# Attention over more than 1024 keys: the second map's first half takes its exponential by its own maximum

## The chip, the cores and the metric

The kernel runs on one core of one Trainium2 chip. The metric is the device time of one execution in microseconds; the kernel before is given by the median of three runs. One further execution was taken by the hardware profiler, and every duration below comes from that one.

## The reference

One inference step of a small decoder, for a prompt of 2048 tokens and 8 samples of 8 tokens with cached keys and values. Layer 0 is a pooling mixer beside differential attention, layer 1 is gated linear attention. The change is in the prompt's differential attention. Per head (4 of them) and block of 128 queries, with two query/key maps of 64 dimensions and values of 128:

```python
sc = jnp.einsum('bqhcd,bkhcd->bhcqk', qi, k)              # c: the two maps
sc = jnp.where((qpos[:, None] >= kpos[None, :])[None, None, None], sc, -jnp.inf)
p = jax.nn.softmax(sc, axis=-1)
a = p[:, :, 0] - lam_full * p[:, :, 1]
return jnp.einsum('bhqk,bkhe->bqhe', a, v)
```

The result is normalised per head, multiplied by a gate and projected. A softmax row is the same whatever number is taken from the scores before the exponential, so long as sum and exponentials use the same one. All of it is fp32; products are split in parts for accuracy.

## The kernel before

The attention works in units: one query tile t of 128 queries (0 to 15) and one head h. A unit's keys are nk = 128 (t + 1). `scores` makes the two maps c = 0 and 1 of a unit, `pv` transposes the combined map and multiplies it by the values, two units later. `units` runs over t and, within it, over the heads of a stage. There are three stages: head 0 while the pool branch's output projection fills in (names zp), head 1 while the samples' attention fills in (ssc, stp, spo), heads 2 and 3 together while the attention's output projection and layer norm fill in (otp, op, oyp). `weave` hands out a stage's main work and its fill in a fixed proportion. The order of the instructions on each engine is then set at build time, by a scheduler that replays the program with its own costs and takes what is ready by priority. The score products, the maxima and the exponentials are written at a raised priority. On the chip each engine runs its list strictly in that order.

A unit is short up to t = 7 (nk at most 1024): each map has at most one PSUM tile. From t = 8 on it is long: each map comes in two halves i = 0 and 1, each a tile `sc` of two PSUM banks. There are two such tiles in all (pool `psc`), used in turn, so a half's products (L561, L562) can begin only when the exponential of the half two places earlier has read its tile. Before the change a long unit does for each map: products of half 0, its negated maximum (L566, VectorE), products of half 1, its maximum, the smaller of the two negated maxima (L579), then the exponential of both halves with that one number (L581, ScalarE), each with its row sum, and the sum of the two row sums (L584). After the second map, the factor c2 = -lambda s1 / s2 is made (L588, L589) and the maps are combined by one instruction over all nk columns, e0 + c2 e1 (L590). `pv` then transposes 128 columns at a time (L613, tile tp), copies four of them to SBUF (L618, ScalarE, tile aT) and multiplies by the values (L606, tile po).

Other lines that are spoken of: L635 squares a unit's result for its norm (VectorE), L40 and L45 split an operand in two parts (L40 is ScalarE's copy, also of the queries qr that `load_q` fetches), L751 transposes the fill's input (loaded from `mixa` to om), L756 is VectorE's part of that operand's split, L816 and L817 are the layer norm's passes on GpSimd, L1520 is a small exponential in the samples' attention.

Of the kernel before, what the change touches and what calls it, by code (L numbers as in the profile page):

```python
# [11 lines left out]
F32 = mybir.dt.float32  # L12
# [4 lines left out]
AF = mybir.ActivationFunctionType  # L17
ALU = mybir.AluOpType
# [412 lines left out]
class Attention:  # L431
# [105 lines left out]
    def scores(self, t, h):  # L537

        nc, sm = self.nc, self.sm
        qh, ql = self.qs[h, t // 2]  # L540
        qs = slice(128 * (t % 2), 128 * (t % 2) + 128)
        nk = 128 * (t + 1)

        npc = 1 if nk <= 512 else 2 if nk <= 1024 else 4
        w = nk // npc
        nt = max(npc // 2, 1)
        nm = sm.tile([128, 2, 2], F32, tag="nm", name=f"nm{t}_{h}", bufs=4)
        s = sm.tile([128, 2, 2], F32, tag="s", name=f"s{t}_{h}", bufs=6)
        places = [self.e.pop(0) for _ in range(2)]
        es = [p.tile([128, NP], F32, tag="e", name=f"e{t}_{h}_{c}") for c, p in enumerate(places)]  # L550
        for c in range(2):
            kst, pieces = self.kst[h][c], []
            for i in range(nt):
                if npc > 1 or c == 0:
                    p = self.sc_tile(f"sc{t}_{h}_{c}_{i}")
                with self.tc.high_priority(300):
                    for j in range(min(npc, 2)):
                        k = 2 * i + j
                        o = p[:, j if npc > 1 else c, :w]
                        ks = slice(k * w, (k + 1) * w)  # L560
                        nc.tensor.matmul(o, qh[:, c, qs], kst[:, ks], start=True, stop=False)  # L561
                        nc.tensor.matmul(o, ql[:, c, qs], kst[:, ks], start=False, stop=k < npc - 1)  # L562
                        if k == npc - 1:
                            nc.tensor.matmul(o[:, w - 128:w], self.ident_b, self.mask, start=False, stop=True)
                    if npc > 1:
                        nc.vector.tensor_reduce(out=nm[:, c, i:i + 1], in_=p[:, :, :w], op=ALU.max, axis=AX.XY,  # L566
                                                negate=True)
                    elif c:
                        nc.vector.tensor_reduce(out=nm[:, :, 0], in_=p[:, :, :w], op=ALU.max, axis=AX.X, negate=True)
                if npc > 1:  # L570
                    pieces.append((c, p[:, :, :w],
                                   es[c][:, 2 * i * w:(2 * i + 2) * w].rearrange("p (g w) -> p g w", g=2)))
                if i < nt - 1:
                    yield 4 * max(w, 256) / 2.4
            if npc == 1 and c:
                pieces = [(c, p[:, c, :w], es[c][:, :w]) for c in range(2)]
            with self.tc.high_priority(300):
                if nt == 2:
                    nc.vector.tensor_tensor(out=nm[:, c, 0:1], in0=nm[:, c, 0:1], in1=nm[:, c, 1:2], op=ALU.min)  # L579
                for i, (m, p, o) in enumerate(pieces):  # L580
                    nc.scalar.activation(o, p, AF.Exp, bias=nm[:, m, 0:1],  # L581
                                         accum_out=s[:, m, i if npc > 1 else 0:][:, :1])
                if nt == 2:
                    nc.vector.tensor_tensor(out=s[:, c, 0:1], in0=s[:, c, 0:1], in1=s[:, c, 1:2], op=ALU.add)  # L584
            if c == 1:
                s1, s2 = s[:, 0, 0:1], s[:, 1, 0:1]
                c2 = sm.tile([128, 1], F32, tag="c2", name=f"c2{t}_{h}", bufs=6)
                nc.vector.reciprocal(out=c2, in_=s2)  # L588
                nc.vector.scalar_tensor_tensor(out=c2, in0=s1, scalar=self.nlam, in1=c2, op0=ALU.mult, op1=ALU.mult)  # L589
                nc.vector.scalar_tensor_tensor(out=es[0][:, :nk], in0=es[1][:, :nk], scalar=c2, in1=es[0][:, :nk],  # L590
                                               op0=ALU.mult, op1=ALU.add)
                self.e.append(places[1])
                self.cur = (es[0], s1, places[0])
            yield 2 * min(npc, 2) * max(w, 256) / 2.4
# [1195 lines left out]
```

## Time and profile before

| | us |
|---|---|
| median of 3 runs | 2233.23 (2230.89 to 2234.32) |
| profiled execution, its time | 2228.95 |
| profiled execution, its span | 2227.0 |
| long units of head 0 | 617 to 750 of the span |
| head 1 | 750 to 910 |
| short units of heads 2 and 3 | 910 to 997 |
| long units of heads 2 and 3 | 997 to 1231 |
| granted TensorE clock, mean | 0.983 |

In the profile PE is TensorE's matmul, PEld its weight load, DVE VectorE, ACT ScalarE, POOL GpSimd, SP SyncE, which issues loads. A row of the timeline gives start, duration, engine, line, operation and tiles, and in brackets how long the engine was idle before it and what released it. A row of waits gives total us, times and the longest. A row of groups gives busy us and mean ns, then idle us ahead of it. A line's row gives least, median and largest ns.

### The profile page before, as it was taken

To read this page: it belongs to the slowest core of one execution; us is meant where nothing else is said; L and a number is where in the kernel's file an instruction comes from. 1 tells how busy PE (TensorE), PEld (TensorE's weight loads), DVE (VectorE), ACT (ScalarE), POOL (GpSimd) and SP (SyncE) were. 2 spreads that over 40 slices of the span, in tenths; PEclk is the share of its full clock that TensorE was granted. 3 is DMA by queue.
4 is the path that set the end of the run, shared out by engine and by line. 5 is a ranking of instruction groups with operands and counts; after the bars stand their busy time and mean duration, and the time that the engine had idled before them with its cause. 6 is when DMAs were issued, how large, how long until landed. Compare 5 with 4: busy or idle time off the path is not lost. (4 is left out here: it accounts for less than half of the span.)

```text
span 2227.0 us, 31576 instructions
## 1 busy us (share of the span) xinstructions
PE 2116.1 (95%) x11777; PEld 1750.0 (79%) x11777; DVE 1131.5 (51%) x2326; ACT 676.3 (30%) x1398; POOL 657.7 (30%) x702
## 2 busy tenths in 40 slices
PE   8999999999999999798889899999999997999997
PEld 7888888878788777677777688888888885877776
DVE  7444511012566676896677654810100127789984
ACT  2111100111433555655565311401111124333441
POOL 0000000231454432665533400000003343555654
PEclk9999999999999999899999999999999998999999
DMA  7311133225855498653322444311211246455522
GB/s 265 123 50 41 44 92 108 71 80 165 247 166 157 143 302 275 181 148 110 102 93 76 147 149 129 129 66 52 83 69 66 81 142 208 149 168 175 168 88 73
DMA packets 202597, 288.51 MB, mean 130 GB/s; under 512 B 30818, under 2 KB 121314, under 8 KB 202434
## 3 DMA queue, kind: packets, MB, share of 16 engines
q1 hardware_dynamic: 166594, 225.30, 33.4%
q0 software_dynamic: 12688, 43.00, 5.1%
q10 hardware_dynamic: 23152, 18.09, 2.5%
q8 instruction: 95, 1.56, 0.3%
q14 instruction: 68, 0.56, 0.1%
HBM read 183.95 MB, written 102.38 MB: 129 GB/s over the span
## 5 line engine op out<-in xcount | busy, mean ns | idle before, releaser
L51 PE MATMUL pm<-xh,wh 128*128 128x512 f32 (+2 forms) x640 | 227.1, 358 | 7.1 <-ACT xh L40 6.7
L53 PE MATMUL pm<-xh,wl 128*128 128x512 f32 (+2 forms) x640 | 228.5, 357 | 0.5 <-DVE wl L45 0.5
L52 PE MATMUL pm<-xl,wh 128*128 128x512 f32 (+2 forms) x640 | 228.0, 356 | 0.6 <-DVE xl L45 0.6
L53 PE MATMUL vt<-wk,yl 128*128 128x512 f32 (+1 forms) x544 | 211.4, 389 | 0.0
L52 PE MATMUL vt<-wk,yh 128*128 128x512 f32 (+1 forms) x544 | 211.3, 390 | 0.0
L51 PE MATMUL vt<-wk,yh 128*128 128x512 f32 (+1 forms) x544 | 208.8, 390 | 0.0
L581 ACT ACTIVATE e<-sc,nm 128x896 f32<-128x896 f32 (+11 forms) x192 | 164.8, 864 | 97.9 <-DVE nm L579 65.9
L1031 POOL TENSOR_TENSOR ve<-ve,nw 128x512 f32<-128x512 f32 (+1 forms) x34 | 45.2, 1330 | 467.9 <-ACT ve L1030 467.9
L45 DVE TENSOR_TENSOR wk<-wr,wk 128x1024 fp32r<-128x1024 f32 x28 | 35.5, 1267 | 273.2 <-ACT wk L40 272.8
L566 DVE TENSOR_REDUCE nm<-sc 128x1 f32<-128x768 f32 (+7 forms) x160 | 156.5, 991 | 29.2 <-PE sc L562 20.0
L606 PE MATMUL po<-vt,aT 128*128 128x128 f32 x1088 | 156.4, 283 | 3.7 <-ACT aT L618 3.0
L397 POOL TENSOR_TENSOR et<-et,gw 128x512 f32<-128x512 f32 (+1 forms) x17 | 22.2, 1304 | 455.3 <-ACT et L396 455.3
L561 PE MATMUL sc<-kst,qh 128*128 128x512 f32 (+9 forms) x352 | 134.1, 384 | 20.7 <-ACT e L581 20.1
L606 PEld LDWEIGHTS po<-vt,aT 128*128 128x128 f32 x1088 | 140.5, 197 | 10.6 <-ACT aT L618 4.0
L51 PEld LDWEIGHTS pm<-xh,wh 128*128 128x128 f32 x640 | 120.9, 189 | 24.8 <-ACT xh L40 6.7
L52 PEld LDWEIGHTS pm<-xl,wh 128*128 128x128 f32 x640 | 120.9, 189 | 19.4 <-DVE xl L45 1.6
L53 PEld LDWEIGHTS pm<-xh,wl 128*128 128x128 f32 x640 | 120.9, 189 | 18.8 <-DVE wl L45 1.0
L562 PE MATMUL sc<-kst,ql 128*128 128x512 f32 (+9 forms) x352 | 122.4, 351 | 0.0
L52 PEld LDWEIGHTS vt<-wk,yh 128*128 128x128 f32 (+1 forms) x544 | 100.4, 185 | 23.0
L53 PEld LDWEIGHTS vt<-wk,yl 128*128 128x128 f32 (+1 forms) x544 | 100.4, 185 | 23.0
L51 PEld LDWEIGHTS vt<-wk,yh 128*128 128x128 f32 (+1 forms) x544 | 100.4, 185 | 22.9
L52 PE MATMUL qm<-yl,wk 128*128 128x512 f32 (+2 forms) x320 | 114.0, 357 | 3.3 <-DVE yl L45 3.3
(354 smaller groups left out, 5074.1 us busy)
## 6 DMA issues: line engine op xcount, KB each, us to landing
sk<-in_cachek SPq DMA_DIRECT2D x64, 256.0 KB
sv<-in_cachev SPq DMA_DIRECT2D x64, 256.0 KB
wr<-in_w_tm SPq DMA_DIRECT2D x24, 512.0 KB
wr<-in_w_fm SPq DMA_DIRECT2D x22, 512.0 KB
wr<-in_w_out SPq DMA_DIRECT2D x16, 512.0 KB
kr<-k SPq DMA_DIRECT2D x32, 256.0 KB
qr<-q SPq DMA_DIRECT2D x64, 128.0 KB
zx<-in_x SPq DMA_DIRECT2D x32, 256.0 KB
```

The lines of the kernel that those rows point to most:

```text
L45: return h, (lo_eng or nc.vector).tensor_tensor(out=lo, in0=raw, in1=hi, op=ALU.subtract)
L51: nc.tensor.matmul(ps, lh(k), rh(k), start=(first and k == 0), stop=False)
L52: nc.tensor.matmul(ps, lh(k), rl(k), start=False, stop=False)
L53: nc.tensor.matmul(ps, ll(k), rh(k), start=False, stop=(last and k == n - 1))
L397: nc.gpsimd.tensor_tensor(out=e, in0=e, in1=gw[:n], op=ALU.mult)
L561: nc.tensor.matmul(o, qh[:, c, qs], kst[:, ks], start=True, stop=False)
L562: nc.tensor.matmul(o, ql[:, c, qs], kst[:, ks], start=False, stop=k < npc - 1)
L566: nc.vector.tensor_reduce(out=nm[:, c, i:i + 1], in_=p[:, :, :w], op=ALU.max, axis=AX.XY, negate=True)
L581: nc.scalar.activation(o, p, AF.Exp, bias=nm[:, m, 0:1], accum_out=s[:, m, i if npc > 1 else 0:][:, :1])
L606: nc.tensor.matmul(po, s[:, 128 * j:128 * j + 128], vt[:, k0 + j, :], start=(k0 + j == 0), stop=(k0 + j == n - 1))
L1031: nc.gpsimd.tensor_tensor(out=e[:n], in0=e[:n], in1=nw[:n], op=ALU.mult)
```

## The change

In a long unit, the first half of the second map no longer waits for the second half's maximum. Its exponential is taken by its own maximum as soon as that is there, at the raised priority (L575 of the changed kernel). The minimum of both negated maxima goes to a third column (L584), which the other exponentials use (L586). A new exponential of one column (L591, ScalarE) makes the factor exp(m0 - m) between the two maxima; VectorE forms the second map's sum as s0 times the factor plus s1 in one instruction in place of the plain sum (L592). The factor c2 is made as before, a new product (L601) gives the first half's own c2, and the combination is done by two instructions of nk / 2 columns, each with its own factor (L604). Short units do what they did. Lines behind line 590 are 14 higher in the changed kernel.

```diff
-        nm = sm.tile([128, 2, 2], F32, tag="nm", name=f"nm{t}_{h}", bufs=4)
-        s = sm.tile([128, 2, 2], F32, tag="s", name=f"s{t}_{h}", bufs=6)
+        nm = sm.tile([128, 2, 3], F32, tag="nm", name=f"nm{t}_{h}", bufs=4)
+        s = sm.tile([128, 2, 3], F32, tag="s", name=f"s{t}_{h}", bufs=6)
...
-                    pieces.append((c, p[:, :, :w],
-                                   es[c][:, 2 * i * w:(2 * i + 2) * w].rearrange("p (g w) -> p g w", g=2)))
+                    o = es[c][:, 2 * i * w:(2 * i + 2) * w].rearrange("p (g w) -> p g w", g=2)
+                    if nt == 2 and c == 1 and i == 0:
+
+                        with self.tc.high_priority(300):
+                            nc.scalar.activation(o, p[:, :, :w], AF.Exp, bias=nm[:, c, 0:1], accum_out=s[:, c, 0:1])
+                    else:
+                        pieces.append((c, i, p[:, :, :w], o))
...
                 if nt == 2:
-                    nc.vector.tensor_tensor(out=nm[:, c, 0:1], in0=nm[:, c, 0:1], in1=nm[:, c, 1:2], op=ALU.min)
-                for i, (m, p, o) in enumerate(pieces):
-                    nc.scalar.activation(o, p, AF.Exp, bias=nm[:, m, 0:1],
-                                         accum_out=s[:, m, i if npc > 1 else 0:][:, :1])
-                if nt == 2:
-                    nc.vector.tensor_tensor(out=s[:, c, 0:1], in0=s[:, c, 0:1], in1=s[:, c, 1:2], op=ALU.add)
+                    nc.vector.tensor_tensor(out=nm[:, c, 2:3], in0=nm[:, c, 0:1], in1=nm[:, c, 1:2], op=ALU.min)
+                for m, i, p, o in pieces:
+                    nc.scalar.activation(o, p, AF.Exp, bias=nm[:, m, 2:3] if nt == 2 else nm[:, m, 0:1],
+                                         accum_out=s[:, m, i:i + 1])
+                if nt == 2 and c == 0:
+                    nc.vector.tensor_tensor(out=s[:, 0, 0:1], in0=s[:, 0, 0:1], in1=s[:, 0, 1:2], op=ALU.add)
+                elif nt == 2:
+                    nc.scalar.activation(s[:, 1, 2:3], nm[:, 1, 0:1], AF.Exp, bias=nm[:, 1, 2:3], scale=-1.0)
+                    nc.vector.scalar_tensor_tensor(out=s[:, 1, 0:1], in0=s[:, 1, 0:1], scalar=s[:, 1, 2:3],
+                                                   in1=s[:, 1, 1:2], op0=ALU.mult, op1=ALU.add)
...
-                c2 = sm.tile([128, 1], F32, tag="c2", name=f"c2{t}_{h}", bufs=6)
-                nc.vector.reciprocal(out=c2, in_=s2)
-                nc.vector.scalar_tensor_tensor(out=c2, in0=s1, scalar=self.nlam, in1=c2, op0=ALU.mult, op1=ALU.mult)
-                nc.vector.scalar_tensor_tensor(out=es[0][:, :nk], in0=es[1][:, :nk], scalar=c2, in1=es[0][:, :nk],
-                                               op0=ALU.mult, op1=ALU.add)
+                c2 = sm.tile([128, 2], F32, tag="c2", name=f"c2{t}_{h}", bufs=6)
+                last = c2[:, nt - 1:nt]
+                nc.vector.reciprocal(out=last, in_=s2)
+                nc.vector.scalar_tensor_tensor(out=last, in0=s1, scalar=self.nlam, in1=last, op0=ALU.mult, op1=ALU.mult)
+                if nt == 2:
+                    nc.vector.tensor_tensor(out=c2[:, 0:1], in0=last, in1=s[:, 1, 2:3], op=ALU.mult)
+                for i in range(nt):
+                    ks = slice(i * nk // nt, (i + 1) * nk // nt)
+                    nc.vector.scalar_tensor_tensor(out=es[0][:, ks], in0=es[1][:, ks], scalar=c2[:, i:i + 1],
+                                                   in1=es[0][:, ks], op0=ALU.mult, op1=ALU.add)
```

The scheduler answers with another order on every engine from the first long unit of head 0 to the end of the attention; ahead of that and behind it nothing moves. Three places, all where query tile 8 of head 3 ends and tile 9 of head 2 begins. In a name such as sc_3_1_0 stand head, map and half, then a running number. TensorE, first as it was and then as it is now, from the unit's last score product to the next unit's first:

```order
L564 MATMUL sc_3_1_1_10232<-mask,identb 128x128
L613 MATMUL tp_2_4_10072<-ident,e_2_0_9836 128x128 x4
L606 MATMUL po_2_10046<-vt_8234,aT_2_0_10052 128x128 x4
L751 MATMUL otp_9951<-oident,om_9947 128x128 x2
L751 MATMUL otp_9951<-oident,oq_2_9489 128x128
L751 MATMUL otp_9951<-oident,oq_3_9546 128x128
L606 MATMUL po_2_10046<-vt_8234,aT_2_4_10077 128x128 x4
L613 MATMUL tp_3_0_10150<-ident,e_3_0_9897 128x128 x4
L561 MATMUL sc_2_0_0_10260<-kst_0_8225,qh_4_9828 128x320
```

```order
L564 MATMUL sc_3_1_1_10284<-mask,identb 128x128
L627 MATMUL tp_2_4_10120<-ident,e_2_0_9884 128x128 x4
L620 MATMUL po_2_10094<-vt_8276,aT_2_0_10100 128x128 x4
L51 MATMUL op_0_9683<-wh_8824,oh_9678 128x512
L52 MATMUL op_0_9683<-wl_8825,oh_9678 128x512
L561 MATMUL sc_2_0_0_10314<-kst_0_8267,qh_4_9876 128x320
```

Less work stands between the two units than before; wide products of the fill now follow the next unit's first half. ScalarE at the same place:

```order
L618 ACTIVATE aT_2_0_10052<-tp_2_0_10047 128x512
L773 DMA y0T<-oyt_1_9774 128x4x128
L618 ACTIVATE aT_2_4_10077<-tp_2_4_10072 128x512
L581 ACTIVATE e_3_1_10138,s_3_10136<-sc_3_1_0_10205,nm_3_10135 128x576
L581 ACTIVATE e_3_1_10138,s_3_10136<-sc_3_1_1_10232,nm_3_10135 128x576
L755 ACTIVATE oh_9956<-otp_9951 128x512
```

```order
L632 ACTIVATE aT_2_0_10100<-tp_2_0_10095 128x512
L769 ACTIVATE oh_9678<-otp_9673 128x512
L575 ACTIVATE e_3_1_10189,s_3_10187<-sc_3_1_0_10256,nm_3_10186 128x576
L632 ACTIVATE aT_2_4_10125<-tp_2_4_10120 128x512
L586 ACTIVATE e_3_1_10189,s_3_10187<-sc_3_1_1_10284,nm_3_10186 128x576
L591 ACTIVATE s_3_10187<-nm_3_10186 128x1
```

The second map's first exponential now stands ahead of a copy of transposed columns that it stood behind, and the factor follows the second. VectorE, from tile 8's last maximum on:

```order
L566 TENSOR_REDUCE nm_3_10135<-sc_3_1_1_10232 128x1
L579 TENSOR_TENSOR nm_3_10135<-nm_3_10135 128x1
L584 TENSOR_TENSOR s_3_10136<-s_3_10136 128x1
L588 RECIPROCAL c_3_10243<-s_3_10136 128x1
L589 SCALAR_TENSOR_TENSOR c_3_10243<-s_3_10136,nlam,c_3_10243 128x1
L756 TENSOR_TENSOR ol_9957<-otp_9951,oh_9956 128x512
L635 SCALAR_TENSOR_TENSOR sqq_2_10101,ssq_2_9880<-oq_2_9879 128x128
L590 SCALAR_TENSOR_TENSOR e_3_0_10137<-e_3_1_10138,c_3_10243,e_3_0_10137 128x1152
L566 TENSOR_REDUCE nm_2_10256<-sc_2_0_0_10260 128x1
```

```order
L566 TENSOR_REDUCE nm_3_10186<-sc_3_1_1_10284 128x1
L770 TENSOR_TENSOR ol_9679<-otp_9673,oh_9678 128x512
L584 TENSOR_TENSOR nm_3_10186<-nm_3_10186 128x1
L566 TENSOR_REDUCE nm_2_10310<-sc_2_0_0_10314 128x1
L592 SCALAR_TENSOR_TENSOR s_3_10187<-s_3_10187 128x1
L598 RECIPROCAL c_3_10295<-s_3_10187 128x1
L599 SCALAR_TENSOR_TENSOR c_3_10295<-s_3_10187,nlam,c_3_10295 128x1
L601 TENSOR_TENSOR c_3_10295<-c_3_10295,s_3_10187 128x1
L604 SCALAR_TENSOR_TENSOR e_3_0_10188<-e_3_1_10189,c_3_10295,e_3_0_10188 128x576 x2
```

The next unit's first maximum now stands ahead of the sum, the factors and the combination, behind which it stood before.

More of the change, by code (lines that the diff above doesn't have):

```diff
@@ L575, in scores @@
             if npc == 1 and c:
-                pieces = [(c, p[:, c, :w], es[c][:, :w]) for c in range(2)]
+                pieces = [(c, 0, p[:, c, :w], es[c][:, :w]) for c in range(2)]
             with self.tc.high_priority(300):
                 if nt == 2:
-                    nc.vector.tensor_tensor(out=nm[:, c, 0:1], in0=nm[:, c, 0:1], in1=nm[:, c, 1:2], op=ALU.min)
-                for i, (m, p, o) in enumerate(pieces):
-                    nc.scalar.activation(o, p, AF.Exp, bias=nm[:, m, 0:1],
-                                         accum_out=s[:, m, i if npc > 1 else 0:][:, :1])
```

## The prediction

> **What bounds the kernel now.** I read the page first, then the busy time by stage, then the waits of TensorE in the stage that the change reaches, then single waits in the timeline.
>
> ```profile
> span 2227.0 us, 31576 instructions
> PE 2116.1 (95%) x11777; PEld 1750.0 (79%) x11777; DVE 1131.5 (51%) x2326; ACT 676.3 (30%) x1398; POOL 657.7 (30%) x702
> ```
>
> TensorE is busy for 95% of the span. The change adds and removes no matmul, so it can only give back idle TensorE time, 111 us in all, and only in the stretch in which the long score units run. Times below are us from the span's start; the columns are busy time per engine, granted clock, DMA share and GB/s.
>
> ```profile
> 617.00:750.00 133.00, 133.00 (x745) 112.55 (x744) 86.59 (x166) 50.80 (x109) 65.83 (x95) 1.00 0.50 152
> 750.00:910.00 160.00, 148.52 (x1563) 115.73 (x1562) 108.33 (x301) 93.61 (x232) 60.61 (x106) 0.99 0.82 254
> 910.00:997.00 87.00, 71.41 (x423) 57.62 (x422) 78.17 (x173) 51.89 (x129) 62.74 (x72) 0.90 0.56 162
> 997.00:1231.00 234.00, 208.09 (x1295) 177.42 (x1295) 165.69 (x364) 128.05 (x268) 116.56 (x117) 0.98 0.30 95
> ```
>
> In the first row (long units of head 0) TensorE never rests, since the pool branch's output products fill every gap: no gain there. In the second (head 1) it rests 11.5 us, in the third (short units of heads 2 and 3, whose code path the change leaves alone) 15.6 us, in the fourth (long units of heads 2 and 3) 25.9 us. So the fourth row matters, and some of the second. Who makes TensorE wait, first over the span and then in 997 to 1231:
>
> ```profile
> PE sc L561 <- ACT e L581: 20.1, 20, 3.3
> PE otp L751 <- DMA om<-mixa: 10.8, 9, 2.4
> PE sc L561 <- ACT e L581: 5.7, 7, 1.8
> PE tp L613 <- ACT aT L618: 4.8, 7, 1.1
> PE op L53 <- DVE ol L756: 3.1, 2, 2.0
> ```
>
> Of the 20.1 us of score products waiting for an exponential to free their PSUM buffer, only 5.7 us lie among the long units of heads 2 and 3. Not all of these can go: a wait ahead of a unit's second map is for the first map's exponential, which keeps its old order. The ones ahead of a new unit's first half, where the releaser is the exponential that the change moves, are these:
>
> ```profile
> 848.12 0.46 PE L561 MATMUL sc<-kst,qh 128*128 128x416 f32 x1 [2.72 <-ACT e L581]
> 1027.26 0.41 PE L561 MATMUL sc<-kst,qh 128*128 128x320 f32 x1 [1.18 <-ACT e L581]
> 1140.32 0.47 PE L561 MATMUL sc<-kst,qh 128*128 128x448 f32 x1 [0.39 <-ACT e L581]
> 1150.60 0.48 PE L561 MATMUL sc<-kst,qh 128*128 128x448 f32 x1 [0.89 <-ACT e L581]
> 1196.17 0.50 PE L561 MATMUL sc<-kst,qh 128*128 128x512 f32 x1 [1.80 <-ACT e L581]
> ```
>
> They add up to 6.98 us, and to 4.26 us without the first, which has another cause:
>
> ```profile
> 846.56 0.63 ACT L40 ACTIVATE qh<-qr 128x512 fp32r<-128x512 f32 x1 [4.80 <-DMA qr<-q]
> ```
>
> There ScalarE stood behind a late query load with the exponential queued after it; an earlier exponential helps only if it comes to stand ahead of that copy.
>
> **What the early exponential takes away.** The wait at 1150.60, followed back:
>
> ```profile
> 1146.54 1.09 DVE L566 TENSOR_REDUCE nm<-sc 128x1 f32<-128x896 f32 x1
> 1147.70 1.07 DVE L566 TENSOR_REDUCE nm<-sc 128x1 f32<-128x896 f32 x1
> 1149.27 0.15 DVE L579 TENSOR_TENSOR nm<-nm 128x1 f32<-128x1 f32 x1
> 1149.45 1.01 ACT L581 ACTIVATE e<-sc,nm 128x896 f32<-128x896 f32 x1 [0.35 <-DVE nm L579]
> 1150.45 1.00 ACT L581 ACTIVATE e<-sc,nm 128x896 f32<-128x896 f32 x1
> ```
>
> The first half's maximum is there at 1147.63. Its exponential starts at 1149.45, after the second half's maximum and the minimum of both. With its own maximum it could start near 1147.8, 1.6 us sooner, which is more than three of the four waits and nearly the fourth. The second half's buffer comes free about 1.0 us sooner too, since only one exponential is left after the minimum. Bounds of this term: 0, if the scheduler spends the gain on other things, to -6.98. It does spend some: in the order shown above, the work between a unit's last score product and the next unit's first one shrank. Prices of that work:
>
> ```profile
> 1138.44 1.06 PE L606 MATMUL po<-vt,aT 128*128 128x128 f32 x8
> 1139.33 0.60 PE L613 MATMUL tp<-ident,e 128*128 128x128 f32 x4
> L51 PE MATMUL pm<-xh,wh 128*128 128x512 f32 (+2 forms) x640 | 227.1, 358 | 7.1 <-ACT xh L40 6.7
> ```
>
> Before, 8 transposes, 8 value products and 4 transposes of the fill stood there: 1.2 + 1.06 + 0.6, about 2.9 us. Now 4 transposes, 4 value products and two wide products: 0.6 + 0.53 + 0.72, about 1.85 us. So about 1.0 of the 1.6 us is spent and 0.6 us of slack stays; the work taken from here now stands ahead of the second half's products, where a buffer is also awaited. I take -4.3: the four waits go, the fifth stays with its load.
>
> **What is added.** Prices, from the stage of heads 2 and 3 where there is a choice:
>
> ```profile
> L590 DVE SCALAR_TENSOR_TENSOR e<-e,c,e 128x2048 f32<-128x2048 f32 x2 | 4.7, 2352 | 0.1
> L590 DVE SCALAR_TENSOR_TENSOR e<-e,c,e 128x1024 f32<-128x1024 f32 x2 | 2.6, 1284 | 0.1
> L589 DVE SCALAR_TENSOR_TENSOR c<-s,nlam,c 128x1 f32<-128x1 f32 x17 | 3.8, 226 | 0.2
> L584 DVE TENSOR_TENSOR s<-s 128x1 f32<-128x1 f32 x32 | 9.5, 298 | 33.7 <-ACT e L581 33.5
> L1520 ACT ACTIVATE sf<-snm,sf x8: 284/306/332, 783.3 to 890.7; 128x3 f32<-128x3 f32 x8
> ```
>
> There are 32 long units (4 heads by 8 query tiles). On VectorE each loses one sum (0.30 by its mean here), and gains the weighted sum (0.23), the product for the first half's factor (0.30), and the second combine instruction, 2 x 1.284 - 2.352 = 0.22. Net 0.45 us a unit, 14 us in all, on an engine that is busy 166 of 234 us. On ScalarE each gains one tiny exponential for the factor, nearest row 0.31 us: 10 us in all, where it is busy 128 of 234. Both lie beside TensorE's work as a rule. Each shows only where TensorE waits for what stands behind. VectorE's weighted sum waits for the factor, and behind it in VectorE's queue stand the next unit's second maximum and minimum, for which the next unit's exponentials wait. That is a wait of the old kind (33.5 us of VectorE's idle time is the old sum waiting for its exponential); it ends later by 0.3 us for the factor and sooner by about 1.0 us for the exponential. Cover gone, the extra VectorE work costs 0.45 us at each of the four waits, 1.8 us; the factor costs 0.31 us at each of the 7 waits on a transposed tile (the row for L618 above), 2.2 us. I take +1.8, with bounds 0 and +4.0.
>
> The third term is the order itself. It moves on every engine from the first long unit to the end of attention, the loads on SyncE's queue with it; before and behind, nothing moves. It decides about waits that the change does not mean to touch: 10.8 + 4.8 + 3.1 us in the fourth stage, and the rest of head 1's 11.5 us. No row prices this. A gain is bounded by about half of them, -8 us; a loss of the same kind by +9 us. I see no reason for a sign and take 0.
>
> **Sum:** -4.3 + 1.8 + 0 = -2.5 us on the profiled execution, whose span is 2227.0 us and whose time is 2228.95 us. That execution is 4.3 us under the median shown, 2233.23 us; I carry the difference to the median: 2230.7 us. About 0.2% (4.5 us) is what a measurement here can tell from no change, so this counts as the same.
>
> **Rivals.** *Larger gain.* All 6.98 us of waits go and the clock recovers: in 997 to 1231 the granted clock is 0.98, which is 4.7 us of 234 lost. Without the added cost this gives -11.7; with it about -10, 2223 us. For it: the waits cluster (1135 to 1151 in the rows above), and the stage with most idle time has the lowest clock (0.90). Against it: the idle time that made the 0.90 lies among the short units, and the scheduler has spent part of the slack. [...]
>
> *Slower: GpSimd stretches the new small VectorE instructions.*
>
> ```profile
> 1021.46 2.36 POOL L816 TENSOR_TENSOR oz<-oz,lng 128x1024 f32<-128x1024 f32 x1
> 1021.99 1.97 DVE L635 SCALAR_TENSOR_TENSOR sqq<-oq 128x128 f32<-128x128 f32 x1
> 1023.98 2.35 POOL L817 TENSOR_TENSOR oz<-oz,lnb 128x1024 f32<-128x1024 f32 x1
> 1024.68 1.67 DVE L579 TENSOR_TENSOR nm<-nm 128x1 f32<-128x1 f32 x1
> L579 DVE TENSOR_TENSOR nm<-nm 128x1 f32<-128x1 f32 x32 | 14.1, 442 | 0.2
> ```
>
> The minimum takes 0.15 us alone (1149.27) and 1.67 us under a GpSimd pass; its mean in this stage is 0.44, so 0.29 us over. The maxima, which read PSUM, show no such stretch (1.09 and 1.07 above). The change adds three VectorE instructions a unit that read two SBUF operands and removes one. At +0.29 each, twice net, and 0.45 for themselves, a unit's chain is 1.0 us longer. It decides once it exceeds the 0.6 us of slack left: 0.4 us a unit over 16 units of heads 2 and 3 is 6.4 us, and with 1.8 us of waits that stay, +8: 2241 us. Against it: the early exponential itself no longer hangs on the stretched minimum. [...]
>
> *Nothing comes of it:* the score products start sooner, and TensorE waits as long at the next transpose or fill tile: 0, 2233 us.
>
> **How the numbers follow.** Small gain near -2.5: 0.42 (0.10 of it beyond 0.2%). Larger gain: 0.27. Slower by the stretched chain or an unlucky order: 0.23. Nothing: 0.08. So faster 0.37, same 0.40, slower 0.23. The likeliest's own range is 2226 to 2235 us (-7.0 to +1.8). The range asked for reaches into both others: low 2219 (-7.0 - 8 and about 1 us of the added cost), high 2244 (no wait gone, +1.8 + 9).
>
> **What would show it.** Right: among the long units of heads 2 and 3, the first half's exponential of the second map starts within 0.3 us of its own maximum; TensorE's wait for exponentials in that stage falls from 5.7 us to under 2; 617 to 750 stays fully busy; the span loses what 997 to 1231 loses. The larger gain: the clock there reads 1.00, and waits at transposes fall as well. The slower case: the weighted sum and the factor's product average over 0.4 us, and waits ahead of first-half score products remain. I am wrong if most of the difference arises outside 750 to 1231, or if TensorE's busy time there changes at one clock.

## The result, and the profile after

The changed kernel takes 2249.05 us (median of 4 runs, 2246.7 to 2250.64), the kernel before beside it 2233.78 us (2230.89 to 2236.3). The ratio is 1.0074, 95% interval 1.0056 to 1.0092: slower by 15 us, above the range of the prediction (2219 to 2244). Medians below are over all executions, and ratios leave out the three that ran at a granted clock of 0.70 to 0.75, over 2600 us: one of the kernel before and two of the kernel at 2222.18 us, whose other eight have a median of 2221.0. The head of the page of the changed kernel:

```profile
span 2248.6 us, 31687 instructions
PE 2126.2 (95%) x11777; PEld 1755.1 (78%) x11777; DVE 1153.9 (51%) x2390; ACT 682.9 (30%) x1430; POOL 653.3 (29%) x702
```

The 11777 matmuls are the same. TensorE's idle time (span less busy time) goes from 110.9 to 122.4 us, +11.5. The mean granted clock goes from 0.983 to 0.979, that is 37.9 and 47.2 us of the span lost to a lower clock, +9.3. Together that is 20.8 of the 21.6 us by which the profiled spans differ (roughly, as the clock is given to three digits). Next, where it arises. The two rows below are the stretch from the first score product of tile 8 in head 2 to the last score product of all, first in the kernel before, then in the changed one, there with head 0 ahead of it (columns as in the prediction):

```profile
998.30:1222.30 224.00, 201.06 (x1259) 171.93 (x1258) 157.60 (x345) 122.65 (x257) 108.38 (x110) 0.98 0.31 97
```

```profile
617.00:750.00 133.00, 133.00 (x750) 113.22 (x749) 91.50 (x187) 53.35 (x117) 66.97 (x94) 1.00 0.49 153
1005.10:1243.90 238.80, 207.59 (x1280) 178.12 (x1281) 176.93 (x387) 129.08 (x281) 117.79 (x116) 0.97 0.30 97
```

It is 14.8 us longer, 8.3 of them idle; it also holds 21 more products (1280 after 1259), since the fill reaches it later. The stretch begins 6.8 us later than before, which makes up the 21.6. Head 0 (617 to 750) is as busy as before. What TensorE waits for in this stretch, two rows of the kernel before and then the changed one:

```profile
PE otp L751 <- DMA om<-mixa: 9.9, 8, 2.4
PE op L53 <- DVE ol L756: 1.1, 1, 1.1
PE otp L765 <- DMA om<-mixa: 13.4, 8, 4.1
PE sc L561 <- ACT e L586: 6.8, 6, 2.6
PE op L53 <- DVE ol L770: 6.3, 5, 3.9
PE tp L627 <- ACT aT L632: 2.7, 5, 0.9
PE sc L561 <- ACT e L575: 1.7, 2, 1.5
```

Score products wait 8.5 us for exponentials (6.8 and 1.7) where they waited 5.7. The fill's share of the loss is larger: it waits 13.4 us for its loads after 9.9, and 6.3 for VectorE's part of the split after 1.1. Only the waits at transposes fall, from 4.8 to 2.7. L575 is the early exponential. It starts when it should:

```profile
1164.02 1.08 DVE L566 TENSOR_REDUCE nm<-sc 128x1 f32<-128x896 f32 x1
1165.14 1.01 ACT L575 ACTIVATE e<-sc,nm 128x896 f32<-128x896 f32 x1 [0.88 <-DVE nm L566]
```

It starts 0.04 us behind its own maximum here, and 7 of the 16 in heads 2 and 3 start within 0.12 us. The others stand behind other work in ScalarE's queue, the last of them 2.9 us; the median is 0.5 us, where the kernel before has 2.2. Yet the waits stay, one place further on:

```profile
1027.19 0.40 PE L561 MATMUL sc<-kst,qh 128*128 128x288 f32 x1 [2.64 <-ACT e L586]
1040.07 0.41 PE L561 MATMUL sc<-kst,qh 128*128 128x320 f32 x1 [0.96 <-ACT e L586]
1154.08 0.47 PE L561 MATMUL sc<-kst,qh 128*128 128x448 f32 x1 [1.00 <-ACT e L586]
1162.67 0.47 PE L561 MATMUL sc<-kst,qh 128*128 128x448 f32 x1 [1.50 <-ACT e L586]
1212.11 0.50 PE L561 MATMUL sc<-kst,qh 128*128 128x512 f32 x1 [1.49 <-ACT e L575]
```

Only the last is a wait of the kind that the change attacks, ahead of a unit's first half. The first, second and fourth stand ahead of a second map's first half and the third ahead of a first map's second half: the releaser is an exponential that was not moved. The largest, followed back, with GpSimd beside it:

```profile
1022.37 1.35 DVE L592 SCALAR_TENSOR_TENSOR s<-s 128x1 f32<-128x1 f32 x1
1024.49 1.65 DVE L599 SCALAR_TENSOR_TENSOR c<-s,nlam,c 128x1 f32<-128x1 f32 x1
1026.07 0.14 DVE L584 TENSOR_TENSOR nm<-nm 128x1 f32<-128x1 f32 x1
1026.31 0.74 ACT L586 ACTIVATE e<-sc,nm 128x576 f32<-128x576 f32 x1 [2.33 <-DVE nm L584]
1021.34 2.37 POOL L830 TENSOR_TENSOR oz<-oz,lng 128x1024 f32<-128x1024 f32 x1
1023.78 2.35 POOL L831 TENSOR_TENSOR oz<-oz,lnb 128x1024 f32<-128x1024 f32 x1
```

Both maxima of the next unit's first map are there at 1024.57. The minimum that its exponentials need stands in VectorE's queue behind the old unit's c2, a one-column instruction that takes 1.65 us and ends when the GpSimd pass does. The weighted sum, which stands in place of the plain sum, took 1.35 us ahead of it.

### The profile page after: what moved, and what is told of

Its sections match the earlier page's. It is cut to its first block, busy times and chain, and to the rows that moved or that the text cites. A ratio compares the mean times of both kernels' runs of the same rounds, so it can differ in the third digit from the quotient of the medians.

```text
span 2248.6 us, 31687 instructions
## 1 busy us (share of the span) xinstructions
PE 2126.2 (95%) x11777; PEld 1755.1 (78%) x11777; DVE 1153.9 (51%) x2390; ACT 682.9 (30%) x1430; POOL 653.3 (29%) x702
## 5 line engine op out<-in xcount | busy, mean ns | idle before, releaser
L586 ACT ACTIVATE e<-sc,nm 128x1024 f32<-128x1024 f32 (+11 forms) x160 | 135.6, 851 | 81.7 <-DVE nm L584 52.6
```

Of the source, the lines that this page charges most:

```text
L586: nc.scalar.activation(o, p, AF.Exp, bias=nm[:, m, 2:3] if nt == 2 else nm[:, m, 0:1], accum_out=s[:, m, i:i + 1])
```

## The experiments

Three readings stood at the start. *Place*: the new order puts the output projection's first tile one unit later, so that it does not cover waits. *Cost*: the added instructions on VectorE and ScalarE are the loss. *Early*: the early exponential harms what stands behind it on ScalarE. Two came up on the way. *Stretch*: small VectorE instructions grow under GpSimd. *Draw*: any new order finds other gaps, and the time hangs on the order more than on the change. Ratios are to the kernel before, run alongside.

**The change in some heads only.** The edit, with `h == 0`, `h == 1` or `h >= 2`; the other heads do what they did before:

```diff
+        own = nt == 2 and h == 0
...
-                    if nt == 2 and c == 1 and i == 0:
+                    if own and c == 1 and i == 0:
```

Heads 2 and 3:

> The change in heads 2 and 3 alone. The order up to the first long unit of heads 2 and 3 is then that of the kernel before, so the stretch of short units has its fill where it was. Theory 'place' (the loss comes from the shifted order: the output projection's first tile stands a unit later in the short units of heads 2 and 3, which wait for exponentials uncovered): short-unit stretch as before, exponential waits there about 8.7 us and not 16.5, total between -4 and +4 us of the kernel before. Theory 'cost' (the loss is the added instructions, 0.5 to 1 us a unit on VectorE's chain): 16 of 32 long units carry them, and these are the least covered ones, so most of the loss stays, +8 to +15 us.

2239.28 us, ratio 1.0029 (1.0015 to 1.0043).

Head 0:

> The change in head 0 alone, where TensorE is fully covered by the pool projection. Theory 'place': the order of everything behind shifts all the same; the first output-projection tile has 0 of 24 products at tile 5 of head 3 and 23 at tile 6 of head 2 (before: 24 and 24), so part of the loss in the short units of heads 2 and 3 appears though no instruction was added there: +3 to +10 us. Theory 'cost': head 0 has no idle TensorE time, so 0, within 3 us.

2225.97 us, ratio 0.9975 (0.9961 to 0.9989): faster than both kernels.

Head 1:

> The change in head 1 alone. Theory 'place': as for head 0 alone, fill at tile 5 of head 3 is 0 of 24, at tile 6 of head 2 24: +3 to +10 us, in the short units of heads 2 and 3. Theory 'cost': 8 of 32 units carry the instructions, +2 to +5 us, inside head 1.

2238.24 us, ratio 1.0029 (1.0014 to 1.0043).

By the order, at the start of tile 8 in head 2 the kernel before has done 70 products of the output projection, the changed one 48. With the change in heads 2 and 3 alone it is 70, in head 0 alone 50, in head 1 alone 48. Heads 2 and 3, with 70, are slower than the kernel before, and head 0, with 50, is faster, so *place* falls. Nor does one reading's ranges fit all three: the +7.6 us of heads 2 and 3 lies above *place* and just under *cost*, the -5.7 of head 0 is outside both, and only the +6.5 of head 1 is where *place* had it. The three differences (+7.6, -5.7, +6.5 us) add to 8 us in place of 15, so they are no parts of one sum.

**Everything added, nothing released.** All added instructions, but the second map's first half is exponentiated by the common maximum again, so the factor is always 1:

```diff
-                    if nt == 2 and c == 1 and i == 0:
-                        with self.tc.high_priority(300):
-                            nc.scalar.activation(o, p[:, :, :w], AF.Exp, bias=nm[:, c, 0:1], accum_out=s[:, c, 0:1])
-                    else:
-                        pieces.append((c, i, p[:, :, :w], o))
+                    pieces.append((c, i, p[:, :, :w], o))
...
-                    nc.scalar.activation(s[:, 1, 2:3], nm[:, 1, 0:1], AF.Exp, bias=nm[:, 1, 2:3], scale=-1.0)
+                    nc.scalar.activation(s[:, 1, 2:3], nm[:, 1, 2:3], AF.Exp, bias=nm[:, 1, 2:3], scale=-1.0)
```

> All added instructions kept, but the second map's first half takes its exponential by the common maximum again, after the minimum (the factor is then 1). Theory 'cost': the added work without the gain, so at least the whole loss, +15 us or more. Theory 'place': the order shifts here too and the fill is late in the short units (0 of 24 at tile 5 of head 3, 2 at tile 6 of head 2, as in the change), so +8 to +16 us, nearly all in the short units and little in the long ones. A third theory, that the early exponential itself hurts by standing in ScalarE's queue, expects 0 to +4 us here.

2257.87 us, ratio 1.0106 (1.0083 to 1.013). This is slower than the change itself and above the range of *place*. It speaks for *cost* and against *early*, if the order is left out of account. The next two runs took it into account.

**Another order, not one instruction changed.** Of the kernel before:

```diff
-                with self.tc.high_priority(300):
+                with self.tc.high_priority(400):
```

(and the same where the exponentials are written).

> The kernel before with one number changed: score products, maxima and exponentials are written at a priority of 400 instead of 300. Not one instruction is added, removed or made longer; only the scheduler's order changes, from head 1 on, and with it the output projection's fill comes one tile (24 products) later from tile 5 of head 3 to tile 13, as in the changed kernel. Theory 'order' (the loss of the changed kernel is mostly that its order leaves other gaps uncovered, whatever made the order change): 2238 to 2248 us, TensorE idle up by 5 us or more between 915 and 1262 us. Theory 'cost' (the added instructions make the loss by what they take): within 5 us of the kernel before, 2227 to 2237. Theory 'stretch' (small VectorE instructions with two SBUF operands grow under GpSimd): the same as 'cost' here.

2239.63 us, ratio 1.003 (1.0016 to 1.0043). It is slower by 7 us with the same instructions (only semaphore waits differ in number), in the range given for 'order' and above that for *cost*, so *cost* cannot be all. Idle time rose by only 2.7 us over the span (110.9 to 113.6), less than expected, and between 915 and 1262, where 5 us or more were expected, it fell (48.9 to 46.2); the clock, 0.981, lost 4.6 us more.

**The early exponential alone.** The factor, the weighted sum, the product and the second combination are taken out; the first half is not put right, so the output is another one:

```diff
-                    nc.scalar.activation(s[:, 1, 2:3], nm[:, 1, 0:1], AF.Exp, bias=nm[:, 1, 2:3], scale=-1.0)
-                    nc.vector.scalar_tensor_tensor(out=s[:, 1, 0:1], in0=s[:, 1, 0:1], scalar=s[:, 1, 2:3],
-                                                   in1=s[:, 1, 1:2], op0=ALU.mult, op1=ALU.add)
...
-                    nc.vector.tensor_tensor(out=c2[:, 0:1], in0=last, in1=s[:, 1, 2:3], op=ALU.mult)
-                for i in range(nt):
+                for i in range(1):
```

> The early exponential alone: the first half of the second map by its own maximum, with the plain sum, one c2 and one combine instruction as before. It leaves out the putting right of the first half, so its output is another one. The order of the fill in heads 2 and 3 is nearly that of the changed kernel. Theory 'cost': the added instructions are what is lost, so 2225 to 2231, faster than before by the released tiles. Theory 'order': as slow as the changed kernel within 4 us, 2243 to 2250. Half and half: 2236 to 2242.

2252.19 us, ratio 1.0079 (1.0048 to 1.011): as slow as the whole change, without what it adds. *Cost* does not explain the 15 us, unless this kernel's own order hides a gain. Its longest wait:

```profile
1033.12 5.20 DVE L584 TENSOR_TENSOR nm<-nm 128x1 f32<-128x1 f32 x1
1038.36 0.79 ACT L586 ACTIVATE e<-sc,nm 128x640 f32<-128x640 f32 x1 [5.02 <-DVE nm L584]
1039.29 0.64 PE L561 MATMUL sc<-kst,qh 128*128 128x320 f32 x1 [5.05 <-ACT e L586]
1032.44 2.34 POOL L824 TENSOR_TENSOR oz<-oz,lng 128x1024 f32<-128x1024 f32 x1
1034.75 1.25 POOL L45 TENSOR_TENSOR ql<-qr,qh 128x512 fp32r<-128x512 f32 x1
1035.97 2.33 POOL L825 TENSOR_TENSOR oz<-oz,lnb 128x1024 f32<-128x1024 f32 x1
```

A minimum of one column, 0.15 us alone, takes 5.20 us: until three GpSimd passes that follow each other without a gap are through. TensorE stands 5.05 us for it. Hence *stretch*.

**Small instructions with one tensor operand.** Minimum, sum, weighted sum, c2 and product take their other operands as per-partition scalars; for instance

```diff
-                    nc.vector.tensor_tensor(out=nm[:, c, 2:3], in0=nm[:, c, 0:1], in1=nm[:, c, 1:2], op=ALU.min)
+                    nc.vector.tensor_scalar(out=nm[:, c, 2:3], in0=nm[:, c, 0:1], scalar1=nm[:, c, 1:2], scalar2=None, op0=ALU.min)
```

In the changed kernel:

> The changed kernel with its small VectorE instructions of a long unit (minimum, sum, weighted sum, c2, product for the first half) written with one tensor operand and the other operands as per-partition scalars. Same arithmetic, same count. In the changed kernel the weighted sum takes 0.20 us at the least and 0.69 on average in the long units of heads 2 and 3, the minimum 0.14 and 0.23, the product 0.14 and 0.27. Theory 'stretch': these means fall to within 0.05 us of their least value, and 5 us or more come back, to 2235 to 2243. Theories 'order' and 'cost': means may fall, the time stays within 4 us of the changed kernel, 2245 to 2253, unless the order moves; its fill comes back to the place of before from tile 6 on, so 'order' allows down to 2240.

2240.85 us, ratio 1.0036 (1.0025 to 1.0048). The weighted sum and the minimum, in the long units of heads 2 and 3, in the changed kernel and then in this one:

```profile
L592 DVE SCALAR_TENSOR_TENSOR s<-s 128x1 f32<-128x1 f32 x16 | 11.1, 694 | 7.4 <-ACT e L586 4.9 <-ACT s L591 2.5
L584 DVE TENSOR_TENSOR nm<-nm 128x1 f32<-128x1 f32 x32 | 7.4, 230 | 0.4
```

```profile
L584 DVE TENSOR_SCALAR nm<-nm 128x1 f32<-128x1 f32 x31 | 6.5, 210 | 0.4
L592 DVE TENSOR_SCALAR s<-s 128x1 f32<-128x1 f32 x15 | 4.0, 268 | 3.4 <-ACT s L591 3.3
```

The stretch is gone (694 to 268 ns). 8 us came back, as *stretch* had it; but the order moved too, and 'order' allowed down to 2240, so this run does not decide between them. In the kernel before:

> The kernel before with the same rewriting (minimum, sum and c2 of a long unit with one tensor operand). Nothing else. Its fill lies one tile later in heads 2 and 3, as in the changed kernel. Theory 'stretch': the minimum's mean in the long units of heads 2 and 3 falls from 0.44 us to under 0.2 and 2 to 6 us are gained, 2226 to 2230. Theory 'order': 2236 to 2246 for the later fill. Theory 'cost': no change, 2228 to 2236.

2230.83 us, ratio 0.999 (0.9979 to 1.0001). The minimum's mean fell from 0.44 to 0.21 us, and all of VectorE's busy time by 11.7 us (1131.5 to 1119.8), for 1.4 us of the whole, which is not told from none. The time is where 'no change' had it, above *stretch* and below 'order'. Its fill also lies at 48 products, and it is no slower: *place* falls again. (Over all twenty kernels the four with 70 or 72 products average a ratio of 1.0063, the sixteen with 48 or 50 one of 1.0039.)

**The changed kernel in another order.** Priority 400 in all three places:

> The changed kernel, instruction for instruction, in another order: priority 400 in place of 300. Theory 'draw' (an order is as good as its gaps happen to be, and the one that came with the change is a poor one): the time moves by 4 us or more from the changed kernel's 2249, to 2232 to 2245. Theory 'early' (the early exponential itself does harm, since ScalarE stands at it until the first half's maximum is there, or since it takes ScalarE from other copies): stays at 2245 to 2253.

2238.21 us, ratio 1.0039 (1.0024 to 1.0053). Same instructions as the changed kernel, 11 us less: *draw* as expected, against *early*.

**The kernel before at 200.**

> The kernel before, instruction for instruction, with priority 200: a second other order of it beside the one at 400 (2239.6). Theory 'draw': moves again, anywhere from 2228 to 2245, and not likely below the kernel before's 2232 by more than 4. If orders of the same instructions agree within 3 us of 2232, the 2239.6 at 400 was an outlier and 'draw' is weaker.

2253.21 us, ratio 1.0107 (1.008 to 1.0135): more than I had allowed. Only semaphore waits differ in number from the kernel before, and its fill stands nearly where it stood (72 products at that point). Its page, and the long units of heads 2 and 3 from the first score product of tile 8 to the last:

```profile
span 2246.2 us, 31580 instructions
PE 2120.1 (94%) x11777; PEld 1753.6 (78%) x11777; DVE 1141.2 (51%) x2326; ACT 676.7 (30%) x1398; POOL 654.1 (29%) x702
...
1001.00:1246.30 245.30, 208.28 (x1260) 178.61 (x1261) 174.77 (x350) 124.92 (x262) 108.97 (x113) 0.95 0.29 90
```

This stretch is 21.3 us longer than before, 14.1 of them idle, with one product more (1260 after 1259): the same stage and the same kind of loss as in the changed kernel, and again scattered waits. The longest of them:

```profile
1124.39 2.35 DVE L584 TENSOR_TENSOR s<-s 128x1 f32<-128x1 f32 x1 [1.31 <-ACT e L581]
1126.98 2.20 DVE L589 SCALAR_TENSOR_TENSOR c<-s,nlam,c 128x1 f32<-128x1 f32 x1
1130.04 1.80 DVE L590 SCALAR_TENSOR_TENSOR e<-e,c,e 128x1536 f32<-128x1536 f32 x1
1131.98 1.09 PE L613 MATMUL tp<-ident,e 128*128 128x128 f32 x4 [4.38 <-DVE e L590]
1124.35 2.38 POOL L816 TENSOR_TENSOR oz<-oz,lng 128x1024 f32<-128x1024 f32 x1
1126.81 2.36 POOL L817 TENSOR_TENSOR oz<-oz,lnb 128x1024 f32<-128x1024 f32 x1
```

The sum (0.30 us by its mean before) and c2 (0.23) take 4.55 us under two GpSimd passes, and the transposes behind them wait 4.38.

**The early exponential alone, with one tensor operand.** The two edits above together (first half not put right):

> The early exponential without the putting right (its output is another one, as in the run with 2252), and the minimum, sum and c2 of a long unit written with one tensor operand. In that run a minimum of 0.15 us took 5.20 us under GpSimd passes with TensorE idle for 5.05 us behind it. Theory 'stretch': 10 us or more come back, 2236 to 2243. Theory 'early': 2246 to 2253. Theory 'draw' alone gives no number, only that it moves.

2222.18 us, ratio 0.9952 (0.9937 to 0.9966): by the ratios 28 us less than the same kernel with two operands, more than any reading had given. The early exponential stands in the fastest kernel of all, so *early* is no loss that comes in every order. Whether the stretch or the new order made the 28 us is not separated.

**Head 0 only, with one tensor operand in all long units.**

> The change in head 0 only (2226.0, where TensorE was covered all along) and the small VectorE instructions with one tensor operand in all long units. Theory 'stretch': adds to the gain, 2219 to 2224. Theory 'draw': the gain in head 0 was an order's luck and is lost as easily, 2226 to 2240.

2235.51 us, ratio 1.0013 (0.9999 to 1.0027): 9.5 us more than with two, as *draw* allowed and *stretch* did not. So *stretch* has no steady price either, though each stretched instruction can be seen.

**Pairs.** Each kernel and its change, at the same priority and with the same operand form. They are not in the same order, but each is one order of its kind. A further reading, *work*, says that the change costs something in every order. At 400 with one operand, the kernel before:

> The kernel before at priority 400, with the small VectorE instructions of a long unit on one tensor operand. The pair of the next run. 'Draw': somewhere in 2225 to 2245, no steady gain over 2239.6. 'Stretch': 2230 to 2236.

2248.86 us, ratio 1.0083 (1.0066 to 1.01), above both expectations. The changed one:

> The changed kernel at priority 400 with one tensor operand. Pairs so far of the same priority and operands (changed less before): +17 us (300), -1.4 (400), +10 (300, one operand). 'Work' (the change costs something in every order): 4 us or more above the run before this one. 'Draw': the difference lies anywhere in -12 to +12.

2243.67 us, ratio 1.0061 (1.0044 to 1.0078), 5 us under its pair: as *draw* allowed, against *work*. The changed kernel at 200:

> The changed kernel at priority 200, where the kernel before took 2253.2. 'Work': 2257 or more. 'Draw': near the changed kernel's own 2249, as its order differs little from that one, so at or under the 2253 of before: 2240 to 2253, the pair's difference below zero.

2258.87 us, ratio 1.0125 (1.0108 to 1.0142): where *work* had it, against *draw*. The kernel before at 100, then the changed one:

> The kernel before at priority 100, a fourth order of the same instructions. 'Draw': 2230 to 2258. If it lies within 3 us of 2232, half of the four orders do, and the kernel before's is an ordinary one; at 2238 or more, its own order is the best of four.

2254.56 us, ratio 1.0115 (1.0098 to 1.0132): the kernel before's own order is the best of the four measured.

> The changed kernel at priority 100; the kernel before there stands at 1.0115 of its own time at 300. Five pairs so far differ by +7.4, +0.9, +1.8, -2.2 and +4.6 thousandths (changed less before). 'Work': 1.0155 or more of the kernel before, 2264 and up. 'Draw' with nothing of its own: 1.004 to 1.019, 2239 to 2272, and a mean of six pairs whose interval holds zero.

2243.3 us, ratio 1.005 (1.0033 to 1.0066): faster than its pair, in the range of *draw* and 21 us under *work*.

| priority, operands | before | changed | changed less before, thousandths |
|---|---|---|---|
| 300, two (the case itself) | 1 | 1.0074 | +7.4 |
| 400, two | 1.0030 | 1.0039 | +0.9 |
| 200, two | 1.0107 | 1.0125 | +1.8 |
| 100, two | 1.0115 | 1.0050 | -6.5 |
| 300, one | 0.9990 | 1.0036 | +4.6 |
| 400, one | 1.0083 | 1.0061 | -2.2 |

The mean is +1.0 with a 95% interval of -4.2 to +6.2 (six pairs, standard deviation 4.9): 2 us, between 9 us faster and 14 us slower. In the rows with two operands, where within a column the order is all that differs, the ratio spreads by 11.5 thousandths before and 8.6 after, 26 and 19 us. What is shown, then, is that a new order with the same instructions can lose as much as the change lost. How much of the 15 us is the order's and how much the change's own is not: the interval reaches to 14.

**Head 0 only, at 400.**

> The change in head 0 only, at priority 400. At 300 it took 2226.0, 0.9975 of the kernel before. The kernel before at 400 takes 1.003. If the change in head 0 has a worth of its own: 0.998 to 1.002, 2227 to 2236. If that gain was its order's: 1.003 or more.

2228.57 us, ratio 0.9984 (0.9972 to 0.9996). Against the kernel before with the same settings, head 0 alone stands at -2.5 (300), -4.6 (400) and +2.3 thousandths (300, one operand). Two of its three kernels beat the kernel before and the changed one, and the one at 300 is the fastest that does the whole computation. The run at 400 fell in the range given for a worth of its own in head 0; whether the change has one there is not settled by three.

## Why the prediction was wrong

**What failed is the third term, the order: "I see no reason for a sign and take 0", with bounds of -8 and +9 us.** The same instructions as before in three other orders take 7, 24 and 26 us more (ratios 1.0030, 1.0107, 1.0115). So this term ranges from half of the whole result to nearly twice it, and its upper bound was too small by a factor of almost three. All three orders lie above the kernel before; of four orders the first is the best by chance once in four, so a sign is hinted at and not shown. I bounded the term by about half of the waits that the old order still had in the fourth stage (half of 18.7 is 9.3; with the rest of head 1, which I named and did not add, it would have been about 14). But a new order makes waits that are not in the old list. In the long units of heads 2 and 3 the wait for loads rose by 3.5 us and that for VectorE's split by 5.2, in work that the change does not touch. Which late load and which stretched instruction fall on the path is decided by where each lands among the others, and that moves with the order; this is read from the waits followed back above, and not shown by a run of its own.

*The early exponential, -4.3.* Right in kind: it starts with its own maximum in 7 of the 16 units, and the waits ahead of first halves fall, from the 4.26 us quoted there to the 1.7 us on L575. So -2.5 rather than -4.3. But the wait for exponentials in the stage was to fall from 5.7 under 2 us and rose to 8.5: it went to the next tiles, whose exponentials still need the minimum of both halves. I had written that the work taken from between the units now stands "ahead of the second half's products, where a buffer is also awaited", and did not price it.

*The added work, +1.8.* Neither shown nor refuted. The early exponential without it is as slow at 300 (1.0079 against 1.0074), and with one operand it is 19 us faster (0.9952 against 1.0036); in each comparison the order differs too, so neither gives a price. The single prices were good for the product (0.27 us for the 0.30 taken) and wrong for the weighted sum, 0.69 us for 0.23.

*The rival of stretched instructions or an unlucky order, 2241 us.* A slower kernel is what came, 8 us slower than that; that the stretch made the difference is not shown. Its first half was seen but priced by a mean excess of 0.29 us, and a mean hides what matters: of the 32 minima of that stage 24 took under 0.2 us, and the longest 2.30; in the runs single small instructions took 5.20 and 5.67 us, and the one of 5.20, which was on the path, cost TensorE 5.05. Its price did not follow the rule of 0.6 us of slack a unit either, since taking the stretch away, in a new order each time, gave by the ratios anything from 28 us less to 12 us more. The contrast with the maxima does hold: the eight over 576 columns in that stage took 0.74 to 0.76 us, beside a GpSimd pass or not. The longest stretch in the rows above, 5.20 us, lasts to the end of the third pass.

*The larger gain* rested on the clock's return. The clock went down instead, 0.983 to 0.979. That the listed waits had lowered it was my estimate. In the kernel before, 997 to 1231 has three stretches of 3.4 us at a clock of 0.50: one behind the listed wait of 1.80 us, two behind waits of 2.42 and 2.26 us for the fill's loads, which the change does not touch. Behind the three listed waits of 0.39 to 1.18 us the clock stayed at 1.00. And the 0.90 of the short units goes with the largest share of idle time (15.6 of 87 us), not with the most of it (25.9 of 234 us, at 0.98). *What was to show me wrong:* most of the difference does arise within heads 1 to 3 (14.8 of 21.6 us in the long units of heads 2 and 3), head 0 stayed busy, and the weighted sum came out over 0.4 us, half of what I had named as the sign of the slower case (the product, at 0.27, did not).

What stays open: which feature of an order makes it good. The place of the fill, the amount of added work and the sum of the stretches were each tried, and none sorts the kernels by time.

## What to carry to other kernels

Where a build-time scheduler sets the order, a small edit is first of all a new order: measure the unchanged instructions in a few other orders before crediting or blaming an edit worth less than their spread (here 19 to 26 us, against an edit whose mean over six pairs is 2). A term that "only reorders" is no zero; its price is that spread, and in all three other orders of the kernel before it pointed upwards. Price a wait not by the mean of the instruction behind which it stands but by its longest cases, and ask which tile is awaited next once the first one comes free.

## What the runs showed of the hardware

A two-column VectorE instruction with two SBUF operands, whose line has a median of 0.16 us, took 5.67 us in the changed kernel, beside a run of three GpSimd passes:

```profile
1043.15 5.67 DVE L1669 TENSOR_TENSOR rmoa<-rmra 128x2 f32<-128x2 f32 x1
1051.13 0.79 PE L53 MATMUL op<-wh,ol 128*128 128x512 f32 x1 [3.88 <-DVE ol L770]
1042.89 2.37 POOL L830 TENSOR_TENSOR oz<-oz,lng 128x1024 f32<-128x1024 f32 x1
1045.22 1.26 POOL L45 TENSOR_TENSOR ql<-qr,qh 128x512 fp32r<-128x512 f32 x1
1046.45 2.35 POOL L831 TENSOR_TENSOR oz<-oz,lnb 128x1024 f32<-128x1024 f32 x1
```

The VectorE instruction ends at 1048.82, the third pass at 1048.80. Such lengths are rare: of the VectorE instructions that write one or two columns between 600 and 1310 us, the longest took 5.67, 3.72 and 2.39 us in this kernel and 2.37, 2.37 and 2.30 in the kernel before; a GpSimd pass over 1024 columns takes 2.35 to 2.37 in the rows above. Written with one tensor operand and per-partition scalars, the minimum and the weighted sum of the changed kernel took 0.21 and 0.27 us on average in the long units of heads 2 and 3, in place of 0.23 and 0.69.

A gap of TensorE of 1.80 us was followed by a stretch at half clock. In the kernel before, the wait of 1.80 us that ends at 1196.17 (quoted in the prediction), the only one over 0.6 us since 1180, is followed by

```profile
1190.00:1196.00 6.00, 4.37 (x33) 3.72 (x31) 5.04 (x10) 3.00 (x7) 5.92 (x5) 1.00 0.00 0
1197.10:1200.50 3.40, 3.40 (x14) 2.57 (x13) 3.33 (x9) 0.83 (x3) 3.24 (x7) 0.55 0.25 93
```

with a clock of 0.55 over 3.4 us (third number from the end). In the changed kernel the 3.88 us gap that ends at 1051.13 goes with twice that:

```profile
1049.60:1056.40 6.80, 5.27 (x12) 4.13 (x13) 4.36 (x15) 1.66 (x4) 1.02 (x3) 0.51 0.20 80
```

From 1051.72 to 1055.99 products of 512 columns start 0.43 us apart there, and two at 1056.74 and 1056.98, at full clock again, 0.24 apart. So, as an estimate from these rows, such a wait can cost nearly as much again by the clock behind it: 3.4 us at half clock is up to 1.7 us, 6.8 up to 3.4. It need not come: the kernel before with one tensor operand has a wait of 2.05 us in this stage,

```profile
1190.76 0.49 PE L561 MATMUL sc<-kst,qh 128*128 128x480 f32 x1 [2.05 <-ACT e L581]
1003.50:1222.00 218.50, 198.89 (x1278) 170.95 (x1278) 160.93 (x352) 123.95 (x262) 110.89 (x111) 1.00 0.32 103
```

and a clock of 1.00 throughout. In the traces of the kernel before and of the changed one, what tells the two outcomes apart is where the gap falls. Between 600 and 2000 us the stretches at half clock, 9 and 11, start in each trace on one grid of 3.41 us and last one to five whole steps of it. The first row below is the step ahead of the half clock in the kernel before. The others are from the changed kernel: the two steps that share the gap of 2.64 us ending at 1027.19, and the one behind them, still at 1.00:

```profile
1194.00:1197.40 3.40, 1.60 (x9) 1.00 (x8) 2.66 (x5) 2.68 (x6) 3.40 (x5) 1.00 0.00 0
1022.50:1025.90 3.40, 2.06 (x18) 1.71 (x16) 3.37 (x4) 0.36 (x2) 3.32 (x2) 1.00 0.67 210
1025.90:1029.30 3.40, 2.11 (x16) 1.88 (x17) 3.37 (x10) 2.57 (x7) 1.07 (x3) 1.00 0.02 5
1029.30:1032.70 3.40, 3.40 (x22) 3.00 (x21) 2.34 (x8) 2.18 (x6) 0.00 (x0) 1.00 0.38 154
```

TensorE was idle for 1.80 us in the first step and for 1.34 and 1.29 in the next two. Over both traces, in the same range, half clock followed none of the 752 steps at full clock with under 1.5 us of idle time, all 17 with over 1.9, and 3 of the 9 in between. So in these two traces it went with the idle time within one step, and a gap of 2.64 us that lay across two steps left the clock at full.
